# An encoder layer on one core: indexer a step later, a fourth scratch tile, the residual scaled on VectorE, attention of a pair begun when key and query are split

## The chip, the cores and the metric

The kernel runs on one core of a Trainium2 chip. The metric is the device time of one execution in microseconds (us), less is better. Before the change it is the median of three runs. Beside it stands one profiled execution, and all rows below are from that one.

The engines are named as the profile names them: PE is TensorE, PEld its loading of the stationary operand, DVE VectorE, ACT ScalarE, POOL GpSimd, SP SyncE, which issues DMAs here. Row names such as `isc` are the program's names for tiles, and `L75` is line 75 of the kernel.

## The reference

One layer of a streaming encoder, for 512 prompt tokens and 32 sample tokens that share the weights (D_MODEL 1024, D_FF 2816):

```python
x = post_norm(x, swiglu(modulate(x, sh1, sc1), f1_gate, f1_up, f1_down), 1.0 + gt1, 0.5, ln1_g, ln1_b)
h = modulate(x, sh2, sc2)
rq, rk, rv, rg, aq, ak, av, iq, ik, iw = mixer_inputs(h, pos, w_in)     # one projection, split, rotated
ret_s, o_ret = retention_prompt(rq, rk, rv)                             # 4 heads of 128, chunks of 64
o_att = dsa_prompt(aq, ak, av, iq, ik, iw)                              # 8 heads of 64
o_ret = (head_norm(o_ret) * silu(rg)).reshape(B, T, RET_WIDTH)
mixed = concatenate([o_ret, o_att], axis=-1)
x = post_norm(x, einsum('btm,md->btd', mixed, w_out), 1.0 + gt2, 1.0, ln2_g, ln2_b)
x = post_norm(x, swiglu(modulate(x, sh3, sc3), f2_gate, f2_up, f2_down), 1.0 + gt3, 0.5, ln3_g, ln3_b)

def post_norm(x, out, gate, weight, g, b):
    return layer_norm(ALPHA * x + weight * gate[:, None, :] * out, g, b)
```

The attention is sparse. An indexer with 8 heads scores every key for every query; only the best 128 keys that the query may see are attended to:

```python
s = einsum('bqhd,bsd->bqhs', iq, ik) * (IDX_DH ** -0.5)
index_score = einsum('bqh,bqhs->bqs', iw, relu(s))                      # then NEG where not admissible
_, idx = lax.top_k(index_score, topk)
logits = einsum('bqhd,bqkhd->bqhk', q, kg) * (ATT_DH ** -0.5)           # kg, vg: keys and values at idx
p = softmax(where(valid, logits, NEG)); out = einsum('bqhk,bqkhd->bqhd', p, vg)
```

The sample tokens do the same against a cache of 512 past keys and values and a given retention state.

## The kernel before

**Layout.** Activations lie with features on the 128 partitions and T = 544 columns (512 prompt, then 32 sample), worked on as two halves of 272 (`HALVES`). For precision each operand of a large product is split into two float32r parts, high and low, and each product is three matmuls (`mm3`, L75). One half of a projection of 128 output features is 24 matmuls, rows `in<-h,wh_w` of 128x272.

**Weights** stream in: SP loads the raw tile, ScalarE casts the high part (L129) and writes its negated copy (L133), and a DMA issued by GpSimd adds the raw weights to that (L134), which makes the low part.

**Order.** The order of TensorE is the order of the code (a manual dependency from each matmul to the next); loads on SP are ordered likewise. Side work stands in generators: `spawn` starts one, `tick`, called after every half of a projection, resumes those that are due, and `yield n` makes one wait n such steps. A dictionary of flags lets one wait for another. So side work falls between two halves of a projection on TensorE. `behind(r, "pe")` ties an instruction of another engine to the last matmul so far, for the scheduler's order alone. On VectorE, ScalarE and GpSimd a scheduler sets the order from there.

**Buffers.** PSUM has eight banks, by tag: three `a`, two `l`, two `t`, one `o`. Projections use the `a` banks in turn. Scratch tiles of 128x544 (`scr`, L55) have three buffers; `vz`, `rl` and what the retention needs take them.

**First place: the indexer.** `queries` splits the rotated index key (`iks`) and four index queries (`iqs`) into parts (casts on ScalarE, L602, the rest on VectorE, L603). The fourth query (`c == 3`) is projected later than the others and takes its own way through the rotation (DMAs into `rp`, then L580 to L584). Then `indexer` runs: for each query tile t it multiplies queries with keys into one `l` and the `o` bank (`isc`), ScalarE applies relu into `rl` (L725), and VectorE sums the heads into a tile `wk` (L730, L732). `topk` then finds the 128 best with rounds of maximum and replacement (L761, L762), two rounds a step, and leaves a mask: flag `("mask", t)`. Meanwhile `retention(hh)` runs for head 0: its key and query projections (`rqk`: ScalarE copies L590 and L591, VectorE L592, GpSimd L595 and L596), a value projection into `vz` (L785), the scores `rs` (two banks, masked by VectorE in L844).

**Second place: attention and gates.** `pair_inputs(c)` is called for four pairs of heads. It projects key and query, spawns `roped` (rotation, split into `aks` and `aqs`), and ends with `value_chunk`, which projects the value and, a step after, transposes it (`vt`, `vts`); then flag `("pair", c)` is set. `attention` works through twelve tiles (c, n), n = 0 to 2, as a pipeline of three stages one step apart: logits (`lg`, two `l` banks; VectorE adds the mask and takes the row maximum, L932; exponential on ScalarE; VectorE scales the rows, L929, all in `Pu`), transposes (`pt`, copied by ScalarE, L1047), values (`po`, split by L970 and L971 into `mx`). A tile starts when its `("pair", c)` and its masks are there. `sample_attention(g)` does two pairs at once for the sample tokens: `sl`, `spt`, `spo` in steps of their own, with the `l` banks for `sl` and `spo`. After the pairs come four gate projections (tanh, L1108). `reload`, spawned at the first of them, brings the layer's input of the residual back into `xq`, and three steps later `residual_next` scales it: GpSimd multiplies by the token's factor (L345, two instructions of 128x544 for two feature tiles), ScalarE scales and adds a constant per feature (L347). Then follow the output projection (`dn<-mx`, summed onto `xq` by L269), a layer norm and the second feed-forward block.

Of the kernel before, what the change touches and what calls it, by code (L numbers as in the profile page):

```python
# [12 lines left out]
AF = mybir.ActivationFunctionType  # L13
ALU = mybir.AluOpType
NOSYNC = mybir.DependencyInfo(mybir.DependencyClass.NoSync, mybir.DependencyReason.DATA)

P = 128
D = 1024
ND = D // P
TP = 512  # L20
TS = 32
T = TP + TS
# [8 lines left out]
HALVES = ((0, HT), (HT, T))  # L31
# [6 lines left out]
def encoder_layer_kernel(ctx, tc, xT, cT, wc1, w_cond, b_condT, lnp, w_gu1, w_dn1, w_in, w_out, w_gu2, w_dn2,  # L38
                         ckT, cv, cikT, s0, cmat, ropes, dec, csm,
                         yT, akT, avT, ikT, st_p, st_s):  # L40
    nc = tc.nc
# [5 lines left out]
    sp = ctx.enter_context(tc.tile_pool(name="sp", bufs=4))  # L47
# [3 lines left out]
    def unit(name, dt=F32):  # L51
        return up.tile([P, 2, T], dt, name=name, tag="u")

    def scr(name, shape=None, dt=F32):
        return sp.tile(shape or [P, T], dt, name=name, tag="s", bufs=3)  # L55

    def half_scr(name, shape=None):
        return sp.tile(shape or [P, HT], F32, name=name, tag="t", bufs=4)
# [23 lines left out]
    flags = set()  # L82
# [7 lines left out]
    def spawn(job):  # L90
        resume(job, now[0] + 1)
# [109 lines left out]
    def xv(xr, d):  # L201
        return xr[d // 2][:, d % 2, :]
# [138 lines left out]
    def residual_next(xr, rs, al, j):  # L341

        for i, (a, b) in enumerate(HALVES):
            rb = rs[i].unsqueeze(1).to_broadcast([P, 2, HT])
            tc.keep_in_program_order(nc.gpsimd.tensor_tensor(xr[j][:, :, a:b], xr[j][:, :, a:b], rb, op=ALU.mult))  # L345
        for d in (2 * j, 2 * j + 1):
            tc.keep_in_program_order(nc.scalar.activation(xv(xr, d), xv(xr, d), AF.Identity, bias=al[1][:, d:d + 1],  # L347
                                                          scale=al[0][:, d:d + 1]))
# [24 lines left out]
    def alpha_ln(n, lg, lb):  # L373
        ag, ab = small(f"ag{n}"), small(f"ab{n}")
        nc.vector.tensor_scalar(ag, lg, ALPHA, None, op0=ALU.mult)
        nc.vector.tensor_scalar(ab, lb, ALPHA, None, op0=ALU.mult)
        return ag, ab
# [29 lines left out]
    xr = [unit(f"xr{j}") for j in range(4)]  # L407
# [42 lines left out]
    for d in range(ND):  # L450
# [5 lines left out]
        if d in (0, 1, 2, 7):  # L456
            n = min(d, 3)
# [11 lines left out]
        x = xv(xr, d)  # L469
        for i in range(2):  # L470
            a0, b0 = HALVES[i]
            f = half_scr("hf")
            for (a, b), r in SEGS[i]:
                nc.vector.tensor_scalar(f[:, a - a0:b - a0], x[:, a:b], g1[:, r, d:d + 1], modT[:, r, d:d + 1],
                                        op0=ALU.mult, op1=ALU.add)
# [65 lines left out]
    al1 = alpha_ln(1, lp[:, 0, :], lp[:, 1, :])  # L541
# [56 lines left out]
    def own(s):  # L598
        return slice(64 * s, 64 * s + 64)
# [7 lines left out]
    def behind(r, kind):  # L607
        if kind in last:
            tc.add_manual_dep(r.ins, last[kind], NOSYNC, reason="pace")
        return r  # L610
# [83 lines left out]
    def queries():  # L694
        yield 2
        parts(iks, ikk)
        for c in range(4):
            if c == 3:
                yield 1
            index_query(c)  # L700
        yield 1
        spawn(indexer())


# [230 lines left out]
    Vs, stacks = {}, {}  # L935

    def pair_inputs(c):
        qk = unit("aqk")
        k, q = qk[:, 0, :], qk[:, 1, :]
        st = [unit("aqs", FR), unit("aks", FR)]  # L940
        V = unit("aV")
        kn = V[:, 1, 64:96]
        qz = V[:, 1, 0:64]
        nc.gpsimd.memset(qz, 0.0)

        rp = unit("rp")

        def roped():
            yield 0
            rope_turn(rp, k, q)  # L950
            nc.sync.dma_start(akT[c], k)
            yield 1
            parts(st[1], k)
            nc.gpsimd.tensor_copy(kn, k[:, TP:T])
            parts(st[0], q)
            for s in range(2):
                nc.gpsimd.tensor_copy(qz[own(s), 32 * s:32 * s + 32], q[own(s), TP:T])

        for slot, z in enumerate((k, q)):
            project(taken(z))  # L960
            rope_gather(rp, slot, z)
        spawn(roped())
        Vs[c] = V
        stacks[c] = st
        value_chunk(V[:, 0, 0:512], V[0:32, 1, 128:256], avT[c], ("pair", c))

    mixed = {}
# [52 lines left out]
    def attention():  # L1020

        GROUPS = (((0, 0, P), (1, P, 3 * P)), ((2, 0, 3 * P),), ((3, 0, TP),))
        tiles = [(c, n) for c in range(4) for n in range(3)]
        pipe = [None] * 3
        pus, outs = {}, {}

        def logits(c, n):
            pair = [bank("l", "lg") for s in range(2)]
            pair_products([[ps[:, a:b] for t, a, b in GROUPS[n]] for ps in pair],
                          [(*stacks[c], t) for t, a, b in GROUPS[n]])  # L1030
            for s, ps in enumerate(pair):
                pus[c, n, s] = unit("Pu")
            for t, a, b in GROUPS[n]:
                for s, ps in enumerate(pair):
                    Pt = pus[c, n, s][:, 0, a:b]
                    mx = sm.tile([P, 1], F32, name="mx", tag="mx")
                    masked(Pt, ps[:, a:b], work[t], mx)
                    softmax_rows(Pt, mx)

        def turn(c, n):  # L1040
            L = GROUPS[n][-1][2]
            for s in range(2):
                pu = pus[c, n, s]
                pt = bank("t", "pt")
                for a in range(0, L, P):
                    turned(pt[:, a:a + P], pu[:, 0, a:a + P], ident)
                nc.scalar.copy(pu[:, 1, :L], pt[:, :L])  # L1047

        def values(c, n):
            if n == 0:  # L1050
                outs[c] = bank("o", "po")
                mixed[4 + c] = unit("mx", FR)
            po, V = outs[c], Vs[c][:, 0, 0:512]
            for t, a, b in GROUPS[n]:
                for kt in range(t + 1):
                    for s in range(2):
                        mm(po[own(s), t * P:(t + 1) * P], V[:, kt * P + 64 * s:kt * P + 64 * s + 64],
                           pus[c, n, s][:, 1, a + kt * P:a + kt * P + P], start=(kt == 0), stop=(kt == t),
                           skip_group_check=True)
            if n == 1:  # L1060
                mixed_part(4 + c, po[:, 0:3 * P], 0, 3 * P)
                flags.add(("att0", c))
            if n == 2:
                mixed_part(4 + c, po[:, 3 * P:TP], 3 * P, TP)
                flags.add(("att", c))

        while tiles or any(pipe):
            item = None
            if tiles:
                c, n = tiles[0]  # L1070
                if flags.issuperset([("pair", c)] + [("mask", t) for t, a, b in GROUPS[n]]):
                    item = tiles.pop(0)
            if pipe[2]:
                values(*pipe[2])
            if item:
                logits(*item)
            if pipe[1]:
                turn(*pipe[1])
            pipe = [item] + pipe[:2]
            yield 1  # L1080
# [8 lines left out]
    def reload():  # L1089
        for j in range(4):  # L1090
            load(xr[j].rearrange("p a t -> p (a t)"), xd[j])
        yield 3
        for j in range(4):
            residual_next(xr, rs1, al1, j)
            yield 1

    rs1 = rs
    for hh in range(4):
        mixed[hh] = unit("mx", FR)
        if hh == 0:  # L1100
            xr = [unit(f"xq{j}") for j in range(4)]
# [192 lines left out]
```

## Time and profile before

| | before |
|---|---|
| median of three runs | 1219.44 us (1221.95, 1219.44, 1215.55) |
| the profiled execution | 1220.04 us, of which the span is 1218.2 us |
| TensorE busy | 1172.8 us, 96% |
| weight load busy (beside the matmuls) | 1132.1 us, 93% |
| VectorE busy | 639.5 us, 52% |
| ScalarE busy | 590.7 us, 48% |
| GpSimd busy | 215.8 us, 18% |
| mean granted TensorE clock | 0.989 of 2.4 GHz |
| HBM traffic over the span | 189 GB/s |

How to read it: an engine is busy while one of its instructions runs. The granted clock is the share of full speed that the chip allowed TensorE; it has two levels, 1.0 (2.4 GHz) and 0.5 (1.2 GHz), so that a mean of 0.989 means that it was at the lower level for a small part of the span. A "wait" names the engine, tile and line that ended it.

### The profile page before, as it was taken

Reading aid. Unit: us, or ns where it says so; the run is one execution under the profiler, and the core shown is the slowest. Engines: PE = TensorE matmul, PEld = TensorE weight load, DVE = VectorE, ACT = ScalarE, POOL = GpSimd, SP = SyncE. Lnnn points to the kernel's source line nnn. Section 1 sums busy time; section 2 is a strip of 40 time slices with the busy share of each in tenths; the row PEclk is TensorE's granted clock in tenths of the full one; section 3 lists DMA queues with packets and bytes.
Section 4 is the critical chain, followed back from the end, with each engine's and each line's share of the span. In section 5 each row is a group of like instructions: output and inputs, shape, how many; then the busy total and the mean of one; then the engine's idle time right before and its main releaser. Section 6 shows DMA issues by size and latency. Waiting matters only on the chain.

```text
span 1218.2 us, 23111 instructions
## 1 busy us (share of the span) xinstructions
PE 1172.8 (96%) x9517; PEld 1132.1 (93%) x9517; DVE 639.5 (52%) x1481; ACT 590.7 (48%) x1004; POOL 215.8 (18%) x243
## 2 busy tenths in 40 slices
PE   6999999999999999799999989999999999999995
PEld 4899999999999899688999978999999999999994
DVE  5655554652547293787897765695632222201416
ACT  2544444443334355654565658646544444433423
POOL 1211111111111302422210131204111111111110
PEclk9999999999999999899999989999999999999998
DMA  9899998896999546644765576934988888888852
GB/s 362 273 306 274 239 262 224 220 235 161 302 263 222 129 175 154 181 119 120 169 133 150 126 241 150 236 100 138 268 185 171 174 175 176 162 173 174 180 87 73
DMA packets 71081, 233.33 MB, mean 192 GB/s; under 512 B 8416, under 2 KB 12256, under 8 KB 70976
## 3 DMA queue, kind: packets, MB, share of 16 engines
q0 software_dynamic: 23760, 84.42, 40.4%
q1 hardware_dynamic: 47216, 147.44, 35.2%
q8 instruction: 74, 1.21, 0.4%
q14 instruction: 31, 0.25, 0.1%
HBM read 222.46 MB, written 7.35 MB: 189 GB/s over the span
## 4 chain that ended last, share of the span: by engine, by line
PE 57%; DVE 4%; DMA 2%; ACT 1%; issue 1%; SPq 0%; DVEq 0%; ACTq 0%
PE gu L75 20%; PE dn L75 16%; PE in L75 14%; PE gu_e L75 1%; PE ro L75 1%; PE lg L75 1%; DMA rp<-iqf 1%; DMA wr_w<-in_w_in 1%; PE po L75 1%; PE pt L78 1%; PE isc L75 1%; PE rs L75 0%; DMA wh_w<-in_w_dn 0%; PE rst L75 0%; DVE xq L296 0%
## 5 line engine op out<-in xcount | busy, mean ns | idle before, releaser
L75 PEld LDWEIGHTS gu<-h,wh_w 128*128 128x128 f32 x3840 | 481.3, 188 | 3.5 <-DMA wh_w<-in_w_gu 1.5
L75 PE MATMUL gu<-h,wh_w 128*128 128x272 f32 x3840 | 482.8, 288 | 1.3 <-DMA wh_w<-in_w_gu 1.3
L75 PE MATMUL dn<-hid,wh_w 128*128 128x272 f32 x2112 | 266.6, 288 | 2.7 <-DMA wh_w<-in_w_dn 2.7
L75 PEld LDWEIGHTS dn<-hid,wh_w 128*128 128x128 f32 x2112 | 265.2, 188 | 3.5 <-DMA wh_w<-in_w_dn 2.9
L129 ACT CAST wh_w<-wr_w 128x1024 fp32r<-128x1024 f32 (+1 forms) x162 | 165.4, 1023 | 148.1 <-PE dn L75 102.2
L75 PE MATMUL in<-h,wh_w 128*128 128x272 f32 x1392 | 191.6, 295 | 0.0
L75 PEld LDWEIGHTS in<-h,wh_w 128*128 128x128 f32 x1392 | 180.3, 191 | 6.8 <-issue 3.4
L133 ACT ACTIVATE wh_w<-wh_w 128x1024 fp32r<-128x1024 f32 (+1 forms) x160 | 165.6, 1037 | 2.9
L134 POOL DMA_DIRECT2D wh_w<-in_w_gu x81 | 70.9, 876 | 422.8 <-ACT wh_w L133 369.4
L516 DVE SCALAR_TENSOR_TENSOR ca<-wc,cz,ca 128x1024 f32<-128x1024 f32 x98 | 128.8, 1339 | 30.4 <-DMA wc<-in_w_cond 30.4
L189 DVE TENSOR_TENSOR tnh<-tnh,gu 128x272 f32<-128x272 f32 x81 | 35.4, 437 | 144.1 <-PE gu L75 144.1
L188 DVE SCALAR_TENSOR_TENSOR tnh<-tnh,gu 128x272 f32<-128x272 f32 x80 | 35.0, 437 | 102.8 <-ACT tnh L187 102.7
L187 ACT ACTIVATE tnh<-gu 128x272 f32<-128x272 f32 x80 | 31.8, 398 | 117.7 <-PE gu L75 117.7
L190 ACT CAST hid<-tnh 128x272 fp32r<-128x272 f32 x88 | 36.8, 419 | 99.0 <-DVE tnh L189 99.0
L134 POOL DMA_DIRECT2D wh_w<-in_w_dn x48 | 41.7, 870 | 226.8 <-ACT wh_w L133 210.2
L269 DVE SCALAR_TENSOR_TENSOR xq<-dn,C,xq 128x272 f32<-128x272 f32 (+2 forms) x48 | 18.0, 403 | 104.6 <-PE dn L75 103.1
L191 DVE TENSOR_TENSOR hid<-tnh,hid 128x272 fp32r<-128x272 f32 x88 | 38.6, 440 | 37.8 <-ACT hid L190 37.6
L134 POOL DMA_DIRECT2D wh_w<-in_w_in x29 | 25.3, 874 | 128.3 <-ACT wh_w L133 53.0
L761 DVE MAX8 m<-wk 128x8 f32<-128x544 f32 (+3 forms) x65 | 38.8, 598 | 0.8
L762 DVE MATCH_REPLACE8 wk<-m,wk 128x544 f32<-128x544 f32 (+3 forms) x65 | 38.0, 585 | 0.0
L75 PE MATMUL dn<-mx,wh_w 128*128 128x272 f32 x192 | 25.2, 289 | 0.0
L75 PE MATMUL dn<-mx,wu_w 128*128 128x272 f32 x192 | 24.6, 287 | 0.0
(264 smaller groups left out, 1105.9 us busy)
## 6 DMA issues: line engine op xcount, KB each, us to landing
wr_w<-in_w_gu SPq DMA_DIRECT2D x84, 512.0 KB, 5.1
wh_w<-in_w_gu POOLq DMA_DIRECT2D x81, 512.0 KB, 7.0
wc<-in_w_cond SPq DMA_DIRECT2D x56, 512.0 KB, 6.8
wr_w<-in_w_in SPq DMA_DIRECT2D x33, 512.0 KB, 5.2
wh_w<-in_w_in POOLq DMA_DIRECT2D x29, 512.0 KB, 7.0
wr_w<-in_w_dn SPq DMA_DIRECT2D x32, 448.0 KB, 3.6
wh_w<-in_w_dn POOLq DMA_DIRECT2D x32, 448.0 KB, 5.7
wc<-in_wc SPq DMA_DIRECT2D x16, 512.0 KB, 10.5
```

What stands on the lines that cost most here:

```text
L75: ordered("pe", nc.tensor.matmul(*a, **kw))
L129: c = nc.scalar.copy(hi[:, :n, :], raw[:, :n, :])
L133: nc.scalar.mul(lo[:, :n, :], hi[:, :n, :].bitcast(F32), -1.0)
L134: nc.gpsimd.dma_start(lo[:, :n, :], src, accum_op=ALU.add)
L187: nc.scalar.activation(t, pg, AF.Tanh, scale=0.5)
L188: nc.vector.scalar_tensor_tensor(t, t, 1.0, pg, op0=ALU.add, op1=ALU.mult)
L189: nc.vector.tensor_tensor(t, t, pu, op=ALU.mult)
L190: nc.scalar.copy(hid[:, 0, a:b], t)
L191: nc.vector.tensor_tensor(hid[:, 1, a:b], t, hid[:, 0, a:b].bitcast(F32), op=ALU.subtract)
L516: nc.vector.scalar_tensor_tensor(acc[r], w, c, acc[r], op0=ALU.mult, op1=ALU.add)
L761: behind(nc.vector.max(m8, w), "pe")
L762: nc.vector.match_replace(w, in_to_replace=m8, in_values=w, imm_value=MARK)
```

## The change

Four edits.

1. The fourth scratch buffer: `scr` gets four in place of three.
2. `queries` waits two steps instead of one ahead of `indexer`, which moves every step of the indexer, and of what waits for it, one half projection later in TensorE's order.
3. `reload` no longer calls `residual_next`. It scales one feature tile a step instead of two: two instructions on VectorE (a half each), which multiply by the feature's constant and the token's factor at once, ordered behind the last matmul so far; then ScalarE adds the feature's constant. There are eight such steps instead of four.
4. `pair_inputs` sets a flag `("stack", c)` one step after key and query of pair c are split, and `attention` starts the pair's tiles at this flag instead of at `("pair", c)`. The entries that the tiles look up are written ahead of the projections for it.

```diff
 def scr(name, shape=None, dt=F32):
-        return sp.tile(shape or [P, T], dt, name=name, tag="s", bufs=3)
+        return sp.tile(shape or [P, T], dt, name=name, tag="s", bufs=4)
...
             index_query(c)
-        yield 1
+        yield 2
         spawn(indexer())
...
                 nc.gpsimd.tensor_copy(qz[own(s), 32 * s:32 * s + 32], q[own(s), TP:T])
-
+            yield 1
+            flags.add(("stack", c))
+
+        Vs[c] = V
+        stacks[c] = st
         for slot, z in enumerate((k, q)):
             project(taken(z))
             rope_gather(rp, slot, z)
         spawn(roped())
-        Vs[c] = V
-        stacks[c] = st
         value_chunk(V[:, 0, 0:512], V[0:32, 1, 128:256], avT[c], ("pair", c))
...
-                if flags.issuperset([("pair", c)] + [("mask", t) for t, a, b in GROUPS[n]]):
+                if flags.issuperset([("stack", c)] + [("mask", t) for t, a, b in GROUPS[n]]):
...
         yield 3
-        for j in range(4):
-            residual_next(xr, rs1, al1, j)
+        for d in range(ND):
+            x = xv(xr, d)
+            for i, (a, b) in enumerate(HALVES):
+                behind(nc.vector.scalar_tensor_tensor(x[:, a:b], x[:, a:b], al1[0][:, d:d + 1], rs1[i], op0=ALU.mult,
+                                                      op1=ALU.mult), "pe")
+            nc.scalar.activation(x, x, AF.Identity, bias=al1[1][:, d:d + 1])
             yield 1
```

TensorE at the first place: the retention scores `rs` of head 0, and the products `isc` next to them, as the difference of the two orders.

```order
 L75 MATMUL rs<-rqk 128x512
 L75 MATMUL rs<-rqk 128x384
-L75 MATMUL isc<-iks,iqs 128x384 x6
+L75 MATMUL isc<-iks,iqs 128x256 x12
 L75 MATMUL in<-h_0_4735,wh_w 128x272 x3
 L75 MATMUL in<-h_1_4736,wh_w 128x272 x3
```

Behind `rs` stand now the second twelve products of query tile 1 (those of the third and fourth query) instead of the first six of tile 2; all products of the indexer have moved by one half projection.

ScalarE at the same place (`sw` belongs to the rotation of the retention key, `vz` is the value of head 0, `wh_w` a weight), before:

```order
L591 COPY sw<-in 64x272
L725 ACTIVATE rl<-isc 128x512 x2
L602 CAST iqs<-iqf 128x512
L785 COPY vz<-in 128x272
L725 ACTIVATE rl<-isc 128x512 x2
L129 CAST wh_w<-wr_w 128x1024
```

and after:

```order
L591 COPY sw<-in 64x272
L785 COPY vz<-in 128x272
L602 CAST iqs<-iqf 128x512
L725 ACTIVATE rl<-isc 128x512 x2
L785 COPY vz<-in 128x272
L129 CAST wh_w<-wr_w 128x1024
```

The cast of the fourth query stood between the first two and the next two relus; now it stands ahead of them all.

VectorE at the same place, as the difference (`wk` are the sums of the indexer, `rsA` the masked scores of head 0):

```order
 L730 TENSOR_SCALAR wk_5182<-rl,ix 128x256
-L712 MEMSET wk_5183 64x64
-L732 SCALAR_TENSOR_TENSOR wk_5182<-rl,ix,wk_5182 128x256
-L603 TENSOR_TENSOR iqs<-iqf,iqs 128x512
-L732 SCALAR_TENSOR_TENSOR wk_5182<-rl,ix,wk_5182 128x256 x6
-L734 MEMSET wk_5182 64x64
-L761 MAX m_5560<-wk_5182 128x8
+L732 SCALAR_TENSOR_TENSOR wk_5182<-rl,ix,wk_5182 128x256 x3
 L844 TENSOR_TENSOR rsA<-rs,Dm 128x512
 L844 TENSOR_TENSOR rsA<-rs,Dm 128x384
```

The rest of the fourth query (L603) has moved ahead of the sums; four sums stand ahead of the masked scores instead of eight.

TensorE at the second place: from the value transposes of the last pair on, before,

```order
L75 MATMUL in<-h_7_4742,wh_w 128x272 x3
L78 MATMUL vt<-cm,vz 128x128 x4
L78 MATMUL vts<-cm,vz 32x128
L75 MATMUL po<-Pu,aV 64x128 x8
L75 MATMUL in<-h_0_4735,wh_w 128x272 x3
```

and after:

```order
L75 MATMUL in<-h_7_4742,wh_w 128x272 x3
L78 MATMUL vt<-cm,vz 128x128 x4
L78 MATMUL vts<-cm,vz 32x128
L75 MATMUL lg<-aks,aqs 128x128 x6
L75 MATMUL lg<-aks,aqs 128x256 x6
L75 MATMUL sl<-ck,aV 32x512
L75 MATMUL sl_8347<-aV 32x32
```

The first logits of the last pair stood a gate projection's half further down, behind `spt`; now they follow the transposes at once, and the sample's `sl` follows them.

## Rows read from the trace of the kernel before

**Rows 1.** Waits of TensorE, whole run: total us, times, longest us.

```profile
PE lg L75 <- DVE mx L971: 4.6, 1, 4.6
PE isc L75 <- ACT iqs L602: 3.5, 1, 3.5
...
PE isc L75 <- ACT rl L725: 1.6, 1, 1.6
...
PE isc L75 <- DVE rsB L844: 1.0, 1, 1.0
```

**Rows 2.** Stretches: length, busy PE, PEld, DVE, ACT, POOL, DMA share, PEclk, GB/s.

```profile
491.30:494.35 3.05, 0.00 (x1) 0.01 (x2) 1.76 (x4) 0.67 (x2) 1.88 (x5) 0.51 0.56 152
494.35:498.10 3.75, 3.75 (x17) 3.26 (x18) 3.10 (x7) 2.36 (x4) 0.16 (x1) 0.50 0.93 363
...
724.50:730.10 5.60, 5.60 (x24) 5.16 (x25) 4.26 (x12) 3.93 (x8) 0.96 (x1) 0.50 0.01 3
23.75:27.10 3.35, 3.35 (x17) 3.35 (x16) 0.76 (x4) 0.00 (x0) 0.00 (x0) 0.50 1.04 406
```

**Rows 3.** Timeline of TensorE, first place: start, us, instructions, [wait ahead].

```profile
483.53 0.97 PE L75 MATMUL isc<-iks,iqs 64*128 64x256 f32 x10
...
494.35 1.35 PE L75 MATMUL isc<-iks,iqs 64*128 64x256 f32 x6 [3.47 <-ACT iqs L602]
...
499.86 1.67 PE L75 MATMUL rs<-rqk 128*128 128x512 f32 x4
501.66 0.79 PE L75 MATMUL isc<-iks,iqs 64*128 64x384 f32 x6
502.38 3.29 PE L75 MATMUL in<-h,wh_w 128*128 128x272 f32 x24
```

**Rows 4.** Timelines of ScalarE, VectorE and GpSimd, first place.

```profile
489.61 0.60 ACT L725 ACTIVATE rl<-isc 128x512 f32<-128x512 f32 x1 [2.39 <-POOL rqk L596]
...
493.68 0.62 ACT L602 CAST iqs<-iqf 128x512 fp32r<-128x512 f32 x1 [3.47 <-DMA iqf<-rp]
...
484.59 0.43 DVE L592 TENSOR_TENSOR rqk<-in,tabR 128x272 f32<-128x272 f32 x1
...
494.33 0.73 DVE L603 TENSOR_TENSOR iqs<-iqf,iqs 128x512 fp32r<-128x512 f32 x1 [1.29 <-ACT iqs L602]
494.98 0.99 DVE L732 SCALAR_TENSOR_TENSOR wk<-rl,ix,wk 128x256 f32<-128x256 f32 x2
...
500.91 1.20 DVE L844 TENSOR_TENSOR rsA<-rs,Dm 128x512 f32<-128x512 f32 x2 [1.74 <-PE rs L75]
...
491.43 1.33 POOL L596 TENSOR_TENSOR rqk<-rqk,sw 128x544 f32<-128x544 f32 x1
```

**Rows 5.** Timeline of TensorE, second place.

```profile
724.50 1.30 PE L75 MATMUL lg<-aks,aqs 64*128 64x384 f32 x5 [4.58 <-DVE mx L971]
...
737.10 1.24 PE L75 MATMUL po<-Pu,aV 128*64 128x128 f32 x12 [1.37 <-ACT Pu L1047]
```

**Rows 6.** Timelines of GpSimd, VectorE and ScalarE, second place and ahead of it.

```profile
717.34 8.12 POOL L345 TENSOR_TENSOR xq<-xq,lny 128x544 f32<-128x544 f32 x6
...
718.37 1.70 DVE L929 TENSOR_SCALAR Pu<-Pu,rl 128x128 f32<-128x128 f32 x2
...
687.38 0.29 DVE L929 TENSOR_SCALAR Pu<-Pu,rl 128x128 f32<-128x128 f32 x1
...
714.67 0.39 ACT L1108 ACTIVATE rgt<-in 128x272 f32<-128x272 f32 x1
...
717.66 0.42 DVE L932 CUSTOM_DVE_ANT_0 Pu<-lg,wk 128x256 f32<-128x256 f32 x1
```

**Rows 7.** Timeline of VectorE at two other places.

```profile
631.98 0.29 DVE L932 CUSTOM_DVE_ANT_0 Pu<-lg,wk 128x128 f32<-128x128 f32 x1 [1.71 <-PE lg L75]
...
789.88 1.32 DVE L334 SCALAR_TENSOR_TENSOR ht<-xq,G,lny 128x272 f32<-128x272 f32 x3
```

**Rows 8.** The stretch of the last pair up to the output projection, columns as in Rows 2.

```profile
708.33:749.10 40.77, 34.82 (x312) 30.69 (x311) 26.15 (x73) 29.43 (x63) 13.41 (x11) 0.92 0.59 174
```

## The prediction: what each part should cost and win

> **What bounds the kernel now.** I read the page's shares and slices first: TensorE is busy nearly all of the span, so that only its gaps and the stretches at the low clock can be won. The list of what TensorE waited for names the gaps [rows 1]: 4.6 us at lg for VectorE, 3.5 and 1.6 us at isc for ScalarE, 1.0 us at isc for VectorE. They lie in two places. The stretches [rows 2] add the clock: after each place TensorE, having stood idle, works on at 0.50 of 2.4 GHz (1.2 GHz), for 3.75 us from 494.35 and for 5.60 us from 724.50. The timelines then tell who is late. First place: the first isc of score tile 1 starts at 483.53, the second stops in its middle and goes on at 494.35 [rows 3], when the fourth query has come back from its rotation: its cast on ScalarE runs at 493.68, its rest on VectorE at 494.33 [rows 4]. Second place: lg of the last pair waits 4.58 us until 724.50, po 1.37 us until 737.10 [rows 5]. There GpSimd runs six of its eight residual multiplications from 717.34 to 725.46, and VectorE, which writes the buffers free that lg wants, takes 1.70 us for two scalings of 128x128, against 0.29 us for one while GpSimd rests [rows 6]. I go from the profiled execution, 1220.04 us, 0.6 us above the median.
>
> **The change, first place (indexer a step later, fourth scratch tile).** No work is added; TensorE's order changes, and with it ScalarE's and VectorE's. I walk through the new order with the old durations.
> The value projection now follows the key projection at once, but its bank is read by VectorE until 484.59+0.43=485.02 [rows 4]; as the isc that stood between ended then too, it starts where it did, and TensorE idles 1.5 us from 483.53. It ends at about 488.3 (3.29 us as in [rows 3], with the next one starting a little before). isc of the first two query tiles: 0.97 us for ten, some 1.35 for twelve: 489.7. Second half of the value projection: 492.9. Now rs, which needs the key of head 0: GpSimd is done at 491.43+1.33=492.76 [rows 4], so it just fits. Its first part takes some 0.95 of the 1.67 us [rows 3], to 493.85.
> Here stands the new wait. The second part of rs needs the bank of isc, which ScalarE's rl empties; the order puts that rl behind the cast of the fourth query, which runs 493.68 to 494.30 whatever TensorE does. One rl takes 0.60 us [rows 4]: rs goes on at 494.9, to 495.6. The second isc needs the first rs bank, and VectorE empties it only behind the fourth query's rest (to 495.06), four accumulations (0.99 for two [rows 4], so 2.0) and its own half of 1.20 us: 497.65. isc ends at 498.9. The next projection starts there, instead of at 502.38, when it had one isc of 0.72 us more behind it (501.66 to 502.38 [rows 3]): 502.38-0.72-498.9=2.8 us gained. The 1.0 us at the isc after that [rows 1] falls away, since VectorE now empties the bank of the small rs ahead of the maxima: 3.7 us together.
> Of the 3.8 us from 493.85 to 497.65 TensorE works only 0.7, which is much like the 2.6 us before the clock fell at 491.30. I take it that it falls again. A drop that meets full work lasted 3.35 us at the start of the kernel, from 23.75 [rows 2], and costs half, 1.7. **Gain 2.0 us**; bounds: 3.7 with no drop, 0.3 with one as long as the old, 3.05+3.75=6.8 us.
> The fourth tile costs no time, and takes away a wait of ScalarE, 2.39 us ahead of the rl at 489.61 [rows 4]; the cast of the fourth query ends last there now, so I count nothing for it. The masks also come a step later, and the first lg a step earlier: VectorE stood idle for 1.71 us ahead of the first masked sums [rows 7], behind it lay sample rounds that now come after; I put this at nothing, with a bound of one such idle time, 1.7 us.
>
> **The change, second place (residual on VectorE, attention earlier).** The six GpSimd instructions leave, and every other of VectorE's gets its own pace back. lg of a pair now follows the value transposes, a step earlier, so that the lg that waited 4.58 us stands no longer behind the sample's spo. po's 1.37 us came from ScalarE's copies queued behind biases that waited for GpSimd; those biases now wait for VectorE's scalings, ahead of the copies by a whole projection. The clock's loss, 5.60/2=2.8 us, goes with the gaps. Removed: 4.58+1.37+2.8=8.75 us.
> Added: the sample's sl now comes straight behind the last pair's first lg, and both want the two banks l. They are free when VectorE has read lg four times. In the old order this same string, from tanh at 714.67 to the fourth sum's end, 717.66+0.42=718.08 [rows 6], took 3.4 us; a copy of the transposed value, 0.2, joins it. tanh starts as the transposes do; transposes and lg take 1.55 us by their spacing; sl waits 3.6-1.55=2.0 us. Queued behind are two gate projections, but nothing else of TensorE. A gap of this kind, 1.37 us, left the clock alone. Bounds: 1.5, and 4.58+2.8=7.4, the old wait with its drop.
> The sixteen scalings have no row of their own. The nearest is L334, the same instruction on the same tiles: 1.32 us for three [rows 7], 0.44 each, 7.0 together. VectorE is busy for 26.15 of the 40.77 us from 708.33 to 749.10 [rows 8], a good 5 of it stretched by GpSimd; half of the scalings fall there, 3.5 us, into some 34. So they are hidden, above all as each pair is queued behind the step's masked sums; if the cover is gone, they cost up to 7.0. The eight biases on ScalarE stay as long as they were. **Gain 8.75-2.0=6.75 us**; bounds 1.35 and 7.25.
>
> The Trainium skill (SBUF — State Buffer, section "SBUF: two separate sides") says that VectorE and GpSimd share a pair of ports, which the one that starts first holds for its whole instruction. The 1.70 us agree. It also says that a VectorE instruction in this class can keep GpSimd from writing the descriptors of the DMAs that it issues; by that, the moved scalings would hold up the low halves of the weights. No row of before shows it; it is the last rival.
>
> **Sum.** 2.0+6.75=8.75 us: 1220.04-8.75=**1211.3 us**. Everything after the output projection is a projection stream that TensorE fills by itself, so that nothing gives the gain back there.
>
> **The rivals.**
> Clock stays up at the first place: 3.7 instead of 2.0, 1209.6 us. For it: the gap is broken by 0.7 us of rs. Against: so was the old one.
> VectorE is late at sl: the wait is the old 4.58 us with its drop, 7.4 in all; 8.75-7.4=1.35, with 2.0: 1216.7 us. For it: sl has a chain of seven VectorE and two ScalarE instructions ahead that used to have a projection's time. Against: GpSimd no longer slows them.
> The attention doesn't really begin earlier, since masks and VectorE set its pace: sl and lg wait as before, only po's 1.37 and the first place are won: 1220.04-2.0-1.4=1216.6 us. Against: the 1.71 us idle [rows 7].
> **Slower**: VectorE becomes the bound from the last pair to the output projection. sl waits 7.4 with its drop, the 7.0 of scalings lie open, and the gaps they make bring one more drop of 2.8: 1220.04-10.75+7.4+7.0+2.8=1226.5 us. It decides once VectorE's work there passes the 34 us; 26.15-5+3.5=24.7 speaks against.
> The descriptors wait: 7.0 us of scalings, all of it in front of weights with no cushion: 1218.3 us.
>
> **How the numbers follow.** Forecast 0.50, clock up 0.15, VectorE late 0.22, attention held 0.05, slower 0.06, descriptors 0.02. What a measurement of this kernel tells from no change is about 0.5%, 6.1 us: 1213.3 and 1225.5. The forecast's own case spreads over 1209 to 1215, most of it below 1213.3; with the clock's case 0.58 faster. The cases near 1217 and the rest of the forecast make 0.36 the same, the slower one 0.06. Two in ten may be left out: the range reaches from the bound 1209.1 (3.7 and 7.25), less the runs' own spread of some 2 us, to 1218.
>
> **What would show it.** ScalarE: rl right behind the cast of the fourth query at about 494. TensorE: second isc at 497 to 498, next projection near 499, a low clock of one short stretch behind it. The gap before lg and po gone, a gap of about 2 us before sl, no low clock near it. VectorE's scalings at 0.44 us. GpSimd without L345 until the second feed-forward block. The prediction is wrong if sl waits over 4 us, if the clock falls at both places, or if the first isc waits on something that I haven't seen.

## The result and the profile after

The changed kernel takes 1207.68 us (median of six runs, 1206.12 to 1209.67) against 1218.36 us (six runs, 1215.46 to 1222.39): a ratio of 0.9911, 95% interval 0.9892 to 0.9929, or 10.7 us less. The forecast was 1211.3 us, 8.75 less than the profiled execution, with a range from 1207 to 1218. Profiled, the changed kernel took 1208.92 us, of which the span is 1207.1.

Page of after, busy time by engine:

```profile
PE 1170.0 (97%) x9517; PEld 1130.0 (94%) x9517; DVE 640.9 (53%) x1497; ACT 589.9 (49%) x1004; POOL 204.9 (17%) x235
```

What TensorE waited for in after, as in [rows 1]:

```profile
PE isc L75 <- DVE rsA L844: 2.4, 2, 1.8
PE sl L75 <- issue: 1.9, 1, 1.9
...
PE in L75 <- DVE rqk L592: 1.0, 1, 1.0
...
PE po L75 <- ACT Pu L1049: 0.5, 1, 0.5
...
PE rs L75 <- POOL rqk L596: 0.4, 1, 0.4
```

The waits of lg, and of isc for ScalarE, are gone. In their place stand shorter ones: isc for the masks of `rs`, and sl.

**Where the time went.** Four points that both traces have split the execution: the start of the combined projection's first half that streams its weights, the value transposes of the third retention head, those of the first attention pair, and the first half of the output projection. Timeline of TensorE, before:

```profile
464.75 3.18 PE L75 MATMUL in<-h,wh_w 128*128 128x272 f32 x24
...
575.71 0.60 PE L78 MATMUL vt<-cm,vz 128*128 128x128 f32 x4
...
627.33 0.60 PE L78 MATMUL vt<-cm,vz 128*128 128x128 f32 x4
...
749.10 1.14 PE L75 MATMUL dn<-mx,wh_w 128*128 128x272 f32 x7
```

The same points after:

```profile
462.30 3.18 PE L75 MATMUL in<-h,wh_w 128*128 128x272 f32 x24
...
569.50 0.60 PE L78 MATMUL vt<-cm,vz 128*128 128x128 f32 x4
...
621.15 0.60 PE L78 MATMUL vt<-cm,vz 128*128 128x128 f32 x4
...
737.99 3.19 PE L75 MATMUL dn<-mx,wh_w 128*128 128x272 f32 x24
```

Their differences: the first place, 575.71-464.75=110.96 against 107.20 us, **3.8 us won**; the stretch between the places 51.6 in both; the second place, 749.10-627.33=121.77 against 116.84 us, **4.9 us won**; the rest, up to TensorE's end, 455.3 against 454.9. The two places together give 8.7 us, next to the forecast's 8.75, but split otherwise (2.0 and 6.75 were forecast). Another 2.45 us lie ahead of the first place, where the change does nothing: in that execution of before, the first feed-forward block waited for a weight.

```profile
421.12 2.64 PE L75 MATMUL dn<-hid,wh_w 128*128 128x272 f32 x19 [2.67 <-DMA wh_w<-in_w_dn]
```

**First place after**, timeline of TensorE, as [rows 3]:

```profile
482.13 3.25 PE L75 MATMUL in<-h,wh_w 128*128 128x272 f32 x24 [0.99 <-DVE rqk L592]
485.31 0.97 PE L75 MATMUL isc<-iks,iqs 64*128 64x256 f32 x12
486.22 3.30 PE L75 MATMUL in<-h,wh_w 128*128 128x272 f32 x24
489.92 1.77 PE L75 MATMUL rs<-rqk 128*128 128x512 f32 x4 [0.40 <-POOL rqk L596]
493.51 0.97 PE L75 MATMUL isc<-iks,iqs 64*128 64x256 f32 x12 [1.82 <-DVE rsA L844]
494.41 4.79 PE L75 MATMUL in<-h,wh_w 128*128 128x272 f32 x24
...
500.78 0.80 PE L75 MATMUL isc<-iks,iqs 64*128 64x384 f32 x6 [0.59 <-DVE rsA L844]
```

and of ScalarE and VectorE, as [rows 4]:

```profile
489.25 0.62 ACT L602 CAST iqs<-iqf 128x512 fp32r<-128x512 f32 x1 [3.44 <-DMA iqf<-rp]
489.77 1.08 ACT L725 ACTIVATE rl<-isc 128x512 f32<-128x512 f32 x2
...
492.77 1.15 DVE L844 TENSOR_TENSOR rsA<-rs,Dm 128x512 f32<-128x512 f32 x2
```

**Second place after**, timeline of TensorE, as [rows 5]: the first logits of the last pair follow the transposes, and sl comes behind a gap.

```profile
702.93 0.60 PE L78 MATMUL vt<-cm,vz 128*128 128x128 f32 x4
703.37 0.27 PE L78 MATMUL vts<-cm,vz 128*32 128x128 f32 x1
703.58 0.95 PE L75 MATMUL lg<-aks,aqs 64*128 64x128 f32 x12
706.39 2.31 PE L75 MATMUL sl<-ck,aV 128*32 128x512 f32 x8 [1.86 <-issue]
```

The profile names no releaser for sl's wait ("issue"), but sl starts 0.12 us behind the end of the third masked sum of these logits on VectorE, 705.86+0.41=706.27:

```profile
705.86 0.41 DVE L932 CUSTOM_DVE_ANT_0 Pu<-lg,wk 128x256 f32<-128x256 f32 x1
```

po of the last pair waits no more. One short wait of po has come, at the first pair:

```profile
635.41 0.87 PE L75 MATMUL po<-Pu,aV 128*64 128x128 f32 x10 [0.46 <-ACT Pu L1049]
```

Stretches of after. The columns are those of [rows 2], with one correction to its heading: the third from the right is the clock, and the DMA share stands behind it:

```profile
494.67:498.04 3.37, 3.37 (x17) 3.37 (x17) 0.09 (x1) 3.34 (x5) 0.88 (x1) 0.50 0.77 243
703.58:706.10 2.52, 0.95 (x13) 0.74 (x12) 2.04 (x10) 1.12 (x3) 0.00 (x0) 1.00 1.01 401
706.10:709.55 3.45, 3.16 (x19) 1.98 (x20) 2.01 (x14) 3.45 (x9) 0.00 (x0) 0.53 0.33 124
```

From the projections' start to the output projection the clock fell twice to 1.2 GHz, for some 3.4 us each; before, the two low stretches lasted 6.8 us each, the second from 723.4, within the wait of lg, to 730.3.

### The profile page after: what moved, and what is told of

Its sections match the earlier page's. It is cut to its first block, busy times and chain, and to the rows that moved or that the text cites. A ratio compares the mean times of both kernels' runs of the same rounds, so it can differ in the third digit from the quotient of the medians.

```text
span 1207.1 us, 23118 instructions
## 1 busy us (share of the span) xinstructions
PE 1170.0 (97%) x9517; PEld 1130.0 (94%) x9517; DVE 640.9 (53%) x1497; ACT 589.9 (49%) x1004; POOL 204.9 (17%) x235
## 3 DMA queue, kind: packets, MB, share of 16 engines
q8 instruction: 74, 1.21, 0.4%
## 4 chain that ended last, share of the span: by engine, by line
PE 87%; DVE 5%; DMA 5%; issue 2%; ACT 1%; SPq 0%; POOL 0%; DVEq 0%; ACTq 0%; POOLq 0%
PE gu L75 40%; PE dn L75 23%; PE in L75 13%; PE gu_e L75 2%; DMA wc<-in_wc 1%; DMA wr_w<-in_w_in 1%; PE ro L75 1%; PE po L75 1%; PE pt L78 1%; DMA wh_w<-in_w_gu 1%; DMA rp<-iqf 1%; PE lg L75 1%; PE isc L75 1%; PE cc L75 0%; DMA wh_w<-in_w_dn 0%
```

## The experiments

The table gives, for each kernel that was timed repeatedly, the ratio to runs of before made beside it and the two stretches from its trace, from the same four points. An indexer one step later goes with four scratch tiles, except in after_scr3; sl_banks and best_yield3 also have sl in other banks. The two padded kernels ran once each, for their traces alone, and stand below.

| kernel | indexer | residual | attention | ratio (95%) | first place, us | second place, us |
|---|---|---|---|---|---|---|
| before, first trace | old | GpSimd | pair | 1 | 110.96 | 121.77 |
| before_again | old | GpSimd | pair | 1.0008 (0.9989 to 1.0027) | 110.64 | 121.79 |
| first_only | later | GpSimd | pair | 1.0000 (0.9984 to 1.0015) | 107.16 | 127.81 |
| resid_only | old | VectorE | pair | 0.9968 (0.9956 to 0.9980) | 112.05 | 117.48 |
| stack_only | old | GpSimd | split | 0.9978 (0.9966 to 0.9990) | 112.05 | 118.68 |
| second_only | old | VectorE | split | 0.9946 (0.9926 to 0.9966) | 111.59 | 115.78 |
| after_no_stack | later | VectorE | pair | 0.9959 (0.9946 to 0.9972) | 107.57 | 121.76 |
| after_no_resid | later | GpSimd | split | 0.9935 (0.9918 to 0.9952) | 107.20 | 117.46 |
| after | later | VectorE | split | 0.9911 (0.9892 to 0.9929) | 107.20 | 116.84 |
| after_scr3 | later | VectorE | split | 0.9899 (0.9876 to 0.9922) | 107.15 | 115.42 |
| sl_banks | later | VectorE | split | 0.9899 (0.9876 to 0.9921) | 107.56 | 114.70 |
| best_yield3 | two later | VectorE | split | 0.9907 (0.9889 to 0.9925) | 108.63 | 116.42 |

**before_again**: no edit.

> The kernel before, unchanged, for a second trace of it. Of the 11.1 us between the two profiled executions, 2.45 lie ahead of the first changed place: in the first trace of before, the output of the first feed-forward block waited 2.67 us for a weight. Theory: that wait is chance, so it is not in this trace at that place; the time is 1.00 of before. In the same way the transfer that brings the fourth index query back (iqf<-rp) took 3.5 us from issue to landing there and 1.9 us in the trace after; by the theory that is chance too, and it takes 2 to 3 us here. Rival: both belong to the order of before and stand in this trace again, at 2.7 and 3.5 us.

The wait for a weight was not there, so it is chance. The transfer took 3.5 us again, so that is not chance: the rival held for it.

**first_only**

```diff
-        return sp.tile(shape or [P, T], dt, name=name, tag="s", bufs=3)
+        return sp.tile(shape or [P, T], dt, name=name, tag="s", bufs=4)
...
-        yield 1
+        yield 2
         spawn(indexer())
```

> Only the indexer a step later and the fourth scratch tile. Theory: the two places don't touch each other, so this gives what the traces show from the projections' start to the third retention head, 3.8 us less than before (ratio 0.997), with one low clock of some 3.4 us behind the second isc. Rival one: the trace after was lucky in the transfer of the fourth query; with one of 3.5 us the gain is my 2.0 us (0.998). Rival two: without the attention's part the later masks hold up the first logits, a wait of some 1.7 us ahead of the first lg, and the gain is 2 us or less for that reason.

The 3.8 us at the first place are there to the tenth, though without the low clock that the theory had there, and nothing of them is left in the time: the second place takes 6.0 us more than before. TensorE's waits of this kernel (the first logits of the first pair are not among them and the transfer took 1.9 us, so neither rival is what happened):

```profile
PE lg L75 <- DVE mx L971: 4.5, 1, 4.5
...
PE spo L75 <- ACT xq L347: 2.5, 1, 2.5
...
PE po L75 <- DVE mx L971: 1.9, 1, 1.9
```

and a stretch of it, columns as above:

```profile
721.35:735.00 13.65, 8.54 (x62) 7.12 (x63) 8.22 (x26) 9.51 (x20) 4.78 (x4) 0.50 0.45 117
```

The sample's step moved with the indexer. Its sl now stands behind po, its spo a half projection later, where GpSimd's residual is under way and ScalarE's biases queue; TensorE waits three times, and the clock stays at 1.2 GHz for 13.65 us, behind an earlier drop of 3.4 us at po. The same kernel behind the padding (first_pad, below) took 125.66 us at the second place, 3.9 more than before, with the same three waits.

**second_only**: edits 3 and 4 of the change without the first two.

> Only the residual on VectorE and the attention begun at the split of key and query. Theory: 4.9 us less than before (0.996), what the traces show from the fifth value transposes to the output projection: no wait of lg and po, a wait of about 1.9 us at the last pair's sl, and a low clock of some 3.5 us there. Rival: the sl was as late as it was because the indexer came a step later; then sl waits less here, the clock stays up, and the gain is my 6.75 us (0.9945).

The rival came closer in the size: 6.0 us at the second place, 6.6 us in the time. sl doesn't wait, since it stands behind the values of the third pair; instead the last logits wait 1.65 us behind spo, and the clock didn't stay up: it falls for 3.4 us there.

**resid_only, stack_only**: edit 3 alone, edit 4 alone.

> The kernel before with the residual scaled on VectorE alone; TensorE's order is that of before. Theory: the lost time at the second place was GpSimd's doing, which stretched VectorE's instructions, and not the order's. VectorE's instructions between 718.37 and 724.18 of before would take 3.6 us less at their unstretched length, the scalings add 1.0, so the second lg behind spo waits some 2 us instead of 4.58; po's 1.37 us goes, the low clock is at most half as long: 5 to 6 us less than before (0.9955). Rival, as my prediction had it: the lg waits since it stands behind the sample's spo, so it still waits 4 us or more without the new attention order, and the gain is 1.4 to 2 us (0.9985).

> The kernel before with the attention begun at the split alone; GpSimd keeps the residual. Theory: spo is still followed by logits, now those of the last tile, which want its bank while GpSimd stretches VectorE: the wait stays at 3 to 5 us with its low clock, and the time is that of before within 1.5 us (1.000). Rival: the attention's order is what won at the second place; 3 us or more gained (0.9975).

Both win, 4.3 and 3.1 us at the second place. For the residual the theory held in its mechanism: VectorE's two scalings took 1.70 us while GpSimd worked [rows 6], and 0.46 here,

```profile
716.57 0.46 DVE L929 TENSOR_SCALAR Pu<-Pu,rl 128x128 f32<-128x128 f32 x2
```

and the logits behind spo wait half as long:

```profile
720.49 1.29 PE L75 MATMUL lg<-aks,aqs 64*128 64x384 f32 x5 [2.29 <-DVE mx L971]
```

The low clock did not get shorter (6.8 us), so the gain stayed below the 5 to 6 us. For the attention's order the theory fell, though GpSimd still worked beside it: the wait behind spo went from 4.58 to 2.81 us, po's from 1.37 to 0.5. Only the low clock stayed, at 6.8 us.

**after_no_stack, after_no_resid**: the change without edit 4, and without edit 3.

> The changed kernel without the attention's part: indexer later, four scratch tiles, residual on VectorE. Theory: the attention's order only trades one wait for another (sl behind the logits for the logits behind spo), so this is within 1 us of the changed kernel: 10 us less than before (0.9915). Rival: with the indexer later the attention's order is needed; the wait at po that the kernel with the first place alone had (1.9 us) and one of some 2 us at lg add to a low clock, and it is 3 us or more slower than the changed kernel (0.994).

> The changed kernel with the residual left on GpSimd. Theory: the sample's spo then waits 2 to 4 us for the logits' bank, which VectorE, slowed by GpSimd, empties late, with one or two low clocks; it loses most of the first place's 3.8 us as the kernel with the first place alone did: the time of before within 2.5 us (1.000). Rival: the attention begun earlier has the logits out of the way before GpSimd starts, and 5 us or more are gained (0.996 or below).

Both theories fell, both rivals held. Each edit's worth is what the changed kernel has over the kernel without it. With the indexer later, the attention's order is worth 4.9 us at the second place (121.76 against 116.84), and the residual on VectorE 0.6 (117.46 against 116.84; in the times, 0.9935 against 0.9911 with overlapping intervals). Without edit 4, the value transposes of the third pair wait 1.9 us, po 1.9 and lg 2.4, and the clock is low for 6.8 us. With edit 4 and the later indexer together, no logits stand behind spo at all (with edit 4 alone they do, as in stack_only and second_only), so it matters little that GpSimd slows VectorE there.

**sl_banks**

```diff
-        ps, p2 = bank("l", "sl"), bank("l", "sl2")
+        ps, p2 = bank("a", "sl"), bank("a", "sl2")
```

> The changed kernel, but the sample's first products sl go into two of the three banks that the projections use, instead of the two that the logits use. Theory: sl no longer waits for VectorE's four masked sums, so the 1.86 us and the low clock that follows (1.7 us) go: 3.5 us less than the changed kernel, 14 us less than before (0.9885). Rival: VectorE is the bound there, and the next two gate projections wait for the same bank instead: no more than 1 us gained, with a new wait at in for the reading of sl.

2.1 us less than after at the second place, of the 3.5 expected: the wait and the low clock are gone, and waits of 0.5 us at lg and 0.4 at pt have come. The projections don't wait for sl's banks. So it was the two banks that sl waited for. By the times it is 1.5 us faster than after, which the intervals can't tell apart.

**after_scr3**

```diff
-        return sp.tile(shape or [P, T], dt, name=name, tag="s", bufs=4)
+        return sp.tile(shape or [P, T], dt, name=name, tag="s", bufs=3)
```

> The changed kernel with three scratch tiles instead of four. Theory: the fourth tile is worth nothing, since the cast of the fourth query is what ends last there: the time of the changed kernel within 0.7 us (0.991 of before). Rival: the relu waits for a scratch tile again, as it did 2.39 us in before, and since TensorE's second isc hangs on it here, 1.5 us or more are lost at the first place.

The fourth tile is worth nothing: 107.15 against 107.20 us at the first place. This trace shows something else. sl waits as in after, but it and the projection behind it run at 2.4 GHz:

```profile
707.83 1.44 PE L75 MATMUL sl<-ck,aV 128*32 128x512 f32 x8 [1.86 <-issue]
...
709.26 3.26 PE L75 MATMUL in<-h,wh_w 128*128 128x272 f32 x24
```

The same gap with the same work about it lowered the clock in after and not here, and the second place is 1.4 us shorter for it.

**before_pad** (the sixteen transposes are work that the output does not need)

```diff
+    pad = bank("t", "pad")
+    for _ in range(16):
+        turned(pad[:, 0:P], ident, ident)
     iqf = [unit("iqf") for _ in range(2)]
```

> The kernel before with sixteen transposes of 128x128 added that nothing reads, ahead of the combined projection (some 2 us of TensorE's time), only to shift the place at which TensorE's next 16 KB of instructions are loaded. In all five traces with the old place of the indexer one packet of instructions is loaded 1.0 to 1.2 us after the fourth query's transfer (iqf<-rp) is issued, and the transfer takes 3.4 to 3.8 us; in all five with the indexer a step later that packet comes 0.8 us ahead of the issue, and the transfer takes 1.9 us. Theory: the packet holds the transfer up; here it comes some 2 us or more earlier, the transfer takes 1.9 us, isc waits 1.9 instead of 3.5 us for the cast, and the stretch from the projections' start to the third retention head is 1.6 us shorter than the 111.5 us of the other four. Rival: the transfer is slow for what the engines do at that point in the old order; then it takes 3.4 us or more here too.

In before, the transfers of the stretch from 490 us (target and source, queue, count, KB each, us from issue to landing), and the loading of instructions from 491.25 to 491.5 us (queue: packets, MB, share of 16 engines):

```profile
iqf<-rp SPq DMA_DIRECT2D x1, 68.0 KB, 3.5
...
q8 instruction: 1, 0.02, 28.3%
```

In before_pad the packet comes between 484.5 and 484.75, ahead of the issue at 487.43, and the cast starts 1.95 us after that issue:

```profile
487.43 0.51 SPq L584 DMA_DIRECT2D iqf<-rp  x1
...
489.38 0.62 ACT L602 CAST iqs<-iqf 128x512 fp32r<-128x512 f32 x1 [1.93 <-DMA iqf<-rp]
```

The theory held: with the old order, too, the transfer takes 1.9 us when the packet doesn't fall on it. The single DMA packets in the traces show how it is held up. The transfer goes as 32 packets of 2176 bytes. In before, 30 of them start 1.17 to 1.54 us behind the issue, while the packet of 16384 bytes is under way (1.12 to 2.25 us behind the issue); the last two start at 2.25 and 2.47 us, the first of them just as that packet ends. It is so in all five traces with the slow transfer: two of 32 packets are late, and the first late one starts within 0.02 us of the packet's end. In the nine others all 32 have started by 1.54 us. The stretch is 108.40 us, 2.2 to 3.7 less than the other five of the old order. Not all of that is the packet's. While TensorE works off the transposes, the other engines get 2 us ahead, and ScalarE's casts stand a little otherwise; isc's 1.58 us for `rl` is gone as well.

**first_pad**: as before_pad, 132 transposes, in the kernel of first_only (edits 1 and 2).

> The kernel with the later indexer and the fourth scratch tile alone, with 132 transposes added ahead of the combined projection (some 17 us of TensorE's time, ahead of the stretch that is read), which nothing reads. They are meant to bring the next instruction packet forward to about 1 us behind the issue of the fourth query's transfer; the aim is good to some 1.5 us. Theory: if the packet falls 0 to 1.4 us behind the issue, the transfer takes 3 us or more instead of 1.9, and the stretch from the projections' start to the third retention head is some 1.6 us longer than with the later indexer alone (107.16 us), which would be the gain of 2 us that I forecast; if the packet misses that time, the transfer takes 1.9 us. Rival: the later indexer keeps the transfer at 1.9 us wherever the packet falls.

The packet missed: it came 4.8 us behind the issue, and the transfer took 1.9 us. So the rival isn't decided by a run; the late packets of the five slow transfers speak against it. The stretch was 101.53 us, without any wait at the first place: 17 us of head start for the other engines take all of them away.

**best_yield3**

```diff
-        yield 2
+        yield 3
         spawn(indexer())
```

in the kernel with sl in the projections' banks.

> The kernel with sl in the projections' banks, and the indexer one more step later. Theory: the first isc then stands behind the scores rs and waits some 1.2 us for VectorE's masks, where VectorE now has no sums ahead of them; the two waits of 1.8 and 1.5 us at isc go; 106 us from the projections' start to the third retention head instead of 107.5, nothing lost later, because sl no longer shares banks with the logits: 1.5 us less than with sl in other banks alone (0.989 of before). Rival: as with the first place alone, the sample's step falls on a step that is already full (sl behind the second logits, spo ahead of po), and what is won at the first place is lost at the second, 1 to 3 us there.

The rival held for the second place, which takes 1.7 us more than in sl_banks: a gate projection waits 2.0 us for VectorE, and behind it the clock falls for 3.4 us. But nothing is won at the first place either, which takes 1.1 us more (rs waits 1.6 us for GpSimd, isc 1.3). The indexer can be too late as well as too early. By the ratios sl_banks and after_scr3 are the best of these, but their intervals reach over those of after and best_yield3.

## Why the prediction was right, and where not

**The total** was right by luck, since two errors cancelled: the first place won 3.8 us where 2.0 was forecast, the second 4.9 where 6.75 was.

**First place.** The order of events was as walked through. After the 2.45 us that this trace is ahead: value projection forecast at 482.6, measured 482.13; isc at 485.85 and 485.31; rs "just fits", with a wait of 0.40 us for GpSimd. The low clock, too, came in this trace, a drop of 3.37 us that met a projection. The step that failed is that the cast of the fourth query "runs 493.68 to 494.30 whatever TensorE does": less 2.45 that is 491.23, and it ran at 489.25, 2.0 us earlier. So rs didn't pause for `rl`, the second isc came at 493.51 instead of 495.2, and the next projection at 494.41 instead of 496.45. Of the 2.0 us, 0.5 is an earlier issue of the transfer (487.25 against 490.18 less 2.45), and the rest is that it took 1.9 instead of 3.5 us. It did so in all six timed kernels with the indexer one step later, with two steps and in both padded ones, and took 3.4 to 3.8 in the other five: each time when a packet of instructions was loaded 1.0 to 1.2 us behind its issue. TensorE's stream decides when that packet comes, so what TensorE does did matter. How much of the 3.8 us would be left if the packet fell on the transfer in the new order was not measured.

Two terms of the sum that follow the cast were off as well. The 1.0 us at the isc after did not fall away: it still waits for VectorE, 0.6 us. And the drop, put at 1.7 us, cost next to nothing: in first_only, after_scr3 and sl_banks it didn't come, that isc waited 1.3 to 1.7 us instead, and the place took 107.15 to 107.56 us all the same. Against the five traces of the old order, 110.64 to 112.05 us, the six of the new one win 3.1 to 4.9 us.

**Second place.** Removed was what was said: no wait of lg, none of po at the last pair, though one of 0.46 us came at the first pair's. sl waited 1.86 us, forecast 2.0, by the times for the third masked sum instead of the fourth. The sixteen scalings took 0.49 us each (7.5 in all, forecast 7.0), and TensorE waited for none of them:

```profile
L1098 DVE SCALAR_TENSOR_TENSOR xq<-xq,ag,lny 128x272 f32<-128x272 f32 x16 | 7.5, 494 | 0.0
```

The step that failed is that a gap of this kind "left the clock alone": it fell for 3.45 us, worth 1.7, which is nearly all of the 6.75 less 4.9. The comparison was with po's wait of 1.37 us, and the outcome isn't fixed by the gap: after_scr3 has the same one without the drop, and 6.35 us won.

**What the sum hid.** The prediction put the effect of the later indexer on the second place at nothing, with a bound of 1.7 us at the masks. By itself it costs 6.0 us there (3.9 in first_pad), and first_only is no faster than before. Edits 3 and 4 are also not a sum: 4.3 and 3.1 us alone, 6.0 together, and behind a later indexer 4.9 for edit 4 and 0.6 for edit 3. The forecast walked the one combined order and so needed none of these; told edit by edit, as it partly was, it would have been wrong.

**The rivals.** The clock did not stay up at the first place in after; where it did, nothing was won by it, as told above. VectorE was not late at sl beyond the forecast. The attention did begin earlier: the first logits of the last pair start 0.65 us behind the transposes (702.93 to 703.58), against 5.4 (708.33 [rows 8] to 713.76) before. VectorE did not become the bound. For the descriptors, the prediction applied a rule to instructions that it doesn't cover. The Trainium skill (SBUF — State Buffer, section "SBUF: two separate sides") tells of VectorE keeping GpSimd from writing descriptors for VectorE instructions in a two-port mode; of those with two inputs in SBUF, which the scalings are, it says only that they contend with GpSimd instructions that read SBUF. This trace shows no hold-up: the DMA that GpSimd issued at 741.76, while two scalings ran (741.63 to 742.54), took 0.86 us to issue, as the others did, and 8.7 us to landing, against 9.5 for the same transfer before.

**Left open.** The two places give 8.7 us, the medians differ by 10.7. The interval, 8.7 to 13.2 us, reaches just to it; with the clock up at sl the places give 10.1. The mean granted clocks point the same way. It was 0.990 in the profiled execution of after, but 0.992 to 0.995 in its other five, and 0.986 to 0.990 in the ten of before_again. A stretch of 3.4 us at half the clock takes 0.0014 off the mean (half of 3.4, over 1207), and the trace of after has three of them beside a longer one at its end, one of the three at the kernel's start as in [rows 2]. So by this estimate most executions of after had fewer drops than the profiled one. At which place they were missing isn't known.

## What to carry to other kernels

Moving one job by a step moves all that waits for it: follow the moved job's last dependant (here the sample's sl and spo, some 220 us further on), and try each edit alone and without each other one, since here one was worth nothing alone and 4 us in company. Where two jobs share two accumulator banks, a step that holds both makes TensorE wait for the engine that reads them; here another pair of banks removed a wait of 1.9 us and brought two of 0.4 to 0.5. Waits of 1.4 to 1.9 us lowered the clock in some of these traces and left it alone in others, and a drop can also be hidden by a wait behind it that gets shorter, so price it as a range, not as the outcome of the one trace at hand.

## What the runs showed of the hardware

Loading of TensorE's instructions can hold up a small transfer. The profile's page of before counts 74 packets and 1.21 MB on that queue, so 16.4 KB each; one that was loaded 1.0 to 1.2 us behind the issue of a transfer of 68 KB went with 3.4 to 3.8 us from issue to landing (five traces), against 1.9 us when it came 0.7 us or more ahead, or 4.8 us behind (nine traces). Two of the transfer's 32 packets stood behind it, and started when it ended. That the queue is TensorE's is seen in first_pad: 132 transposes more, and 75 packets instead of 74. The Trainium skill (Runtime: NRT & Kernel Launch, section "Instruction fetch mechanics") says that instructions come in blocks of 16 KiB over a queue of the engine's own, and that the cost of crossing a block is mostly hidden; the size agrees, and no wait of TensorE in the list of before is put down to such a packet. But for a transfer beside it the cost was not hidden.
